# A streaming-encoder block: full-width moving parts beside retention, range sums on ScalarE, low weights three steps later

## The chip, the cores and the metric

The kernel runs on one core of a Trainium2 chip. The metric is the device time of one execution in microseconds (us). Three executions of the kernel before took 1543.58, 1543.76 and 1544.12 us; their median, 1543.76 us, is the time to compare with.

## What is computed

One layer over 512 tokens of width 2048: an RMS norm, one combined projection, a sparse attention mixer and a retention mixer, sigmoid gates, an output projection, a gated embedding and a last norm. What matters here is the middle of it:

```python
h = rmsnorm(x, norm_gain)
proj = h @ w_in
(aq, ak, av, az, iq, ik, iw, rq, rk, rv, rz, ga, gb) = jnp.split(proj, SPLIT_POINTS, axis=-1)
...
b_out = retention_mixer(rq, rk, rv, ret_gn_gain) * jax.nn.silu(rz)
merged = jax.nn.sigmoid(ga) * (a_out @ w_a_out) + jax.nn.sigmoid(gb) * (b_out @ w_b_out)
```

## The kernel before

Every large product is made in float16 from two-part numbers: a weight block `w` is split into a high part `wh` (ScalarE, line 257, with a scale) and a low part `wl` (VectorE, line 143: scaled `w` minus `wh`), and the input likewise into a high and a low half. The moving operand of a product is a tile of 512 columns, 256 of the high half beside 256 of the low half. `wh` multiplies all 512, `wl` the 256 high ones, and the two column halves of the result are added afterwards.

Two projections of 128 outputs each are computed together by `gemm_pair` with seven products in place of eight (a Strassen-like scheme: sums of weight blocks against sums of inputs). Four PSUM banks `v`, `p`, `q`, `r` collect the products. A pair has 14 runs of matmuls, 7 with `wh` and 7 with `wl`, each over 8 slices of the contraction. Runs with `wl` have 8 matmuls of 256 columns. Runs with `wh` have 8 matmuls of 512 columns, or, in a *compact* pair, 16 of 256: the high and the low half go one after the other into the same 256 columns of the bank.

What a pair leaves in PSUM is taken out in `copy` (ScalarE, line 372: a bank into SBUF) and `out` (VectorE). In a compact pair `out` is a single operation of 256 columns (line 1492 with its `done`), in any other it is one of 512 columns (line 378, tile `e_t`) and then one that adds the halves of `e_t` (line 1492):

```python
def out(f, x, y, i, c):
    if compact:
        return done(x[:, LO], y[:, LO], i, c, f)
    t = U("e_t")
    f(t, x, y)
    done(t[:, LO], t[:, HI], i, c)
```

The retention stage computes 8 heads. Each head has three pairs: the keys and queries of the head (called the first pair here), then two pairs of merge gates (the second and the third). `COMPACT = True, False, True` makes the first and the third compact. Beside them run the head's rotation (lines 1182 to 1189), its chunk states (line 1281) and its output norm, and rounds of the top-k search (lines 1082 and 1085) as background work. After the stage come sixteen pairs that are not compact.

The order of the work is written by hand: each engine runs its instructions in program order, and `step()`, called as the matmuls are issued, runs work that was put off with `later(n, f)`. `split_to` makes the next weight unit: it issues `wh` at once, and puts off `rest` (the low part, and a sum of weight blocks at line 268 or a DMA that adds one) by a lag of 1 step; there are three buffers each for `wh` and `wl`, and a unit is split shortly before it is used.

The low part of a weight also writes the sum of its row into a column of the tile `stats` (`accum_out`, in `low_part`). At the end `judge1` looks at the exponents of all columns, and a flag tells whether the values were in a range that the fast arithmetic can hold.

Of the kernel before, what the change touches and what calls it, by code (L numbers as in the profile page):

```python
# [59 lines left out]
    me = 2  # L60


STATS = 704
INDEX_Q = 2.0 ** -12
INDEX_K = 2.0 ** 6
LOGITS = 2.0 ** 10
SCALE_Q, SCALE_K, SCALE_V, SCALE_P = 128.0 ** -0.5 * 2.0 ** 7, 2.0 ** 3, 2.0 ** 3, 2.0 ** 14
EXP_LOW, EXP_HIGH = 124, 134
RET_QK, RET_V, RET_AT, RET_S = 2.0 ** 3, 2.0 ** 3, 2.0 ** -4, 2.0 ** -9
RET_Y = 2.0 ** 5  # L70

# [1 line left out]
def block_kernel(tc, flag, cfg, xT, pT, posb, posq, w_in, w_v, w_r0, w_r1, w_ik, w_a, w_b, w_o, w_ple, w_gate,  # L73
# [7 lines left out]
    with contextlib.ExitStack() as ctx:  # L81
# [41 lines left out]
        if fast:  # L123
            stats = cp.tile([128, STATS], F32, name="stats")
            pool.memset(stats, 1.0)
            one16 = cp.tile([128, 1], F16, name="one16")
            pool.memset(one16, 1.0)
        columns = [0]

        def column(n=1):  # L130
            c = slice(columns[0], columns[0] + n)
            columns[0] += n
            assert columns[0] <= STATS
            return stats[:, c]

        def low_part(l, src, h, gain=None, checked=False):
# [17 lines left out]
        loaded = {}  # L154
        raw_tiles = {}
        unfinished = {}
        state = {"raw": 0, "split": 0, "rate": BG_RATE, "hold": False, "owed": False, "banks": False, "turn": False, "lag": 1}
        in_raws, in_big, added, narrow_raws = set(), set(), set(), set()

        def raw(src, k0, nk, cols, plus=None):  # L160
            raws.append((src, k0, nk, cols, plus))
# [2 lines left out]
        def block(src, chunks, cols=128):  # L164
            ids, k0 = [], 0
            for nk in chunks:
                ids.append(len(units))
                units.append((raw(src, k0, nk, cols), None, nk, cols))
                k0 += nk
            return ids  # L170
# [44 lines left out]
        def view(t, nk, cols):  # L215
            return t.rearrange("p a c -> p (a c)")[:, 0:nk * cols].rearrange("p (a c) -> p a c", c=cols)
# [23 lines left out]
        def split_to(n, lag=None):  # L240
            lag = lag or state["lag"]
            while state["split"] < min(n, len(units)):
                i = state["split"]
                load_to(i + 1)
                r, plus, nk, cols = units[i]
                if r in unfinished:
                    unfinished[r]()
                raw = view(raw_tiles[r], nk, cols)
                if i in in_raws:
                    t = wp.tile([128, 2, 512], cfg.dt, name="whl", tag="wraw", bufs=cfg.raw_bufs)  # L250
                    h, l = t[:, 0:1], t[:, 1:2]
                elif nk * cols == L and i > u_ik[-1]:
                    h, l = (v.rearrange("p (a c) -> p a c", c=cols) for v in both("wh4", "wl4"))
                else:
                    h, l = (view(wp.tile([128, 8, 128], cfg.dt, name=n, tag=n), nk, cols) for n in ("wh", "wl"))
                if i > 0:
                    act.activation(h, raw, AF.Copy, scale=cfg.w)  # L257
                elif fast:
                    dve.tensor_scalar(h, raw, cfg.w, None, op0=OP.mult)
                else:  # L260
                    dve.tensor_copy(h, raw)

                def rest(r=r, plus=plus, l=l, raw=raw, h=h):
                    if unfinished.pop(r, None) is None:
                        return
                    low_part(l, raw, h, cfg.w if fast else None, True)
                    if isinstance(plus, int):
                        dve.tensor_add(raw, raw, view(raw_tiles[plus], nk, cols))  # L268
                    elif plus is not None:
                        later(ADD_LAG if r in in_big and r not in added else 0, lambda: add_block(r, plus))  # L270
                        added.add(r)

                unfinished[r] = rest
                later(lag, rest)
                loaded[i] = (h, l)
                state["split"] += 1
# [8 lines left out]
        def later(n, f):  # L285
            if n <= 0:
                return f()
            tick[1] += 1
            heapq.heappush(soon, (tick[0] + n, tick[1], f))
# [71 lines left out]
        def gemm_pair(ids, X, done, late=False, turned=False, nk=8, more=None, compact=False):  # L361
# [58 lines left out]
            for at, (n, part, ks) in enumerate(runs):  # L420
                at = max(at - early, 0) if late else at
                i, o = ids[n], banks[n]
                if more is not None:
                    more(at)
                elif at in SPLIT_AT and not (late and at == 2):
                    split_to(ids[0] + SPLIT_AT[at], (1 if state["turn"] else 5) if at == 2 else 1)
                if at in LOAD_AT and more is None:
                    load_to(ids[LOAD_AT.index(at)] + AHEAD + LOADS)
                if waiting and state["banks"] and 4 <= at <= 9:
                    bias_banks(waiting.popleft())  # L430
                w, c = loaded[i][part], (ALL, LO)[part]
                begin = ended[n] == 0
                for k in ks:
                    ended[n] += 1
                    x = X[PRODUCTS[n]][k]
                    if turned and isinstance(x, tuple):
                        moving = [(LO, v) for v in x[:2 - part]]
                    elif compact:
                        moving = [(LO, x[:, v]) for v in (LO, HI)[:2 - part]]
                    else:  # L440
                        moving = [(c, x[:, c])]
                    for j, (co, src) in enumerate(moving):
                        pe.matmul(o[:, co], w[:, k], src, start=(n < 4 and begin and k == 0 and j == 0),  # L443
                                  stop=(ended[n] == 2 * nk), skip_group_check=True)
                    count += 1
                    if count % (16 // nk) == 0:
                        step()
                if ended[n] == 2 * nk and n in after:
                    after[n]()
# [194 lines left out]
        PAIRED = [m + 8 * i for m in range(8) for i in range(2)]  # L644
        u_wa.update((m, block(w_a[m], (8,))) for m in PAIRED if m % 8 not in narrow and m not in u_wa)
        u_d = [block_pair(w_o[m], w_o[m + 8]) for m in range(8)]
        u_p = [block(w_ple[:, 8 * q:8 * q + 8], (8,)) for q in range(MF // 4)]
        u_e = [block(w_gate[m], K8) for m in range(cfg.me)]
        u_ep = [block_pair(w_gate[m], w_gate[m + 1]) for m in range(cfg.me, MF, 2)]
# [859 lines left out]
        for h in range(NH):  # L1509
            if fast and h == NH - 1:  # L1510
                state["rate"] = BG_RATES[3]
            if state["rate"] == BG_RATES[2]:
                later(38, lambda: hold(True))
                later(64, lambda: hold(False))
            if fast:
                for n in ROUNDS_IN_HEAD if h else ():
                    later(n, late_round)
            gate_pair(u_r[h], retention(h), COMPACT[0])
            for n in (2 * h, 2 * h + 1):
                d, m = ((sgb, 2 * n), (sga, 2 * n - 16))[n >= 8]  # L1520
                state["turn"] = fast and n == 2 * h
                gate_pair(u_g[n], to(d[m:m + 2], AF.Sigmoid), COMPACT[1 + n % 2])
        state["rate"] = BG_RATES[4]
        state["banks"] = True
        for n, u in enumerate(u_rz):
            y = B("y2")

            def b_out(i, o, y=y, n=n):
                act.activation(o, o, AF.Silu, scale=un_x)
                ov = o.rearrange("p (t i c) -> p t i c", t=4, i=4)  # L1530
                v = y[:, L * i:L * i + L].rearrange("p (i t c) -> p t i c", i=4, t=4)
                pool.tensor_mul(ov, ov, v)
                pool.dma_start(out=bd[2 * n + i], in_=o)

            def y_load(y=y, n=n):
                for i in range(2):
                    sp.dma_start(y[:, L * i:L * i + L], yd[2 * n + i])

            later(16 if n else 0, y_load)
            gate_pair(u, b_out)  # L1540
# [512 lines left out]
        def judge1():  # L2053
            e = cp.tile([128, STATS], I32, name="exps")
            dve.tensor_scalar(e, stats.bitcast(I32), 0x7F800000, 23, op0=OP.bitwise_and, op1=OP.logical_shift_right)
            n = F["n"] = [up.tile([128, 1024], F16, name=v, tag="u")[:, 0:STATS] for v in ("over", "good")]
            dve.tensor_scalar(n[0], e, float(EXP_HIGH), 1000.0, op0=OP.is_gt, op1=OP.mult)
            dve.scalar_tensor_tensor(n[1], e, float(EXP_LOW), n[0], op0=OP.is_ge, op1=OP.subtract)

        def judge2():  # L2060
            F["pe"] = [P("ps_e") for _ in range(2)]
# [151 lines left out]
RET_SPLITS = {("k", 0): 16, ("k", 1): 21, ("q", 0): 18, ("q", 1): 24, ("v", 0): 26, ("v", 1): 37,  # L2213
              ("vd", 0): 40, ("vd", 1): 45}
KEYS_AT = 30, 31
COMPACT = True, False, True
ROUNDS_AT = 19, 44
ROUNDS_IN_HEAD = 15, 44, 106, 106
QK_LOW = 5, 9
# [105 lines left out]
```

## Time and profile before

| what | value |
|---|---|
| median of three executions | 1543.76 us |
| the profiled execution, its own time | 1543.44 us |
| its span, from the first to the last instruction | 1541.6 us |
| TensorE matmul busy | 1529.4 us, 99% |
| VectorE busy | 1317.6 us, 85% |
| ScalarE busy | 970.0 us, 63% |
| GpSimd busy | 225.0 us, 15% |
| mean granted clock of TensorE | 0.998 |

The profile's page gives the busy time of each engine as a share of the span. A matmul's recorded duration is longer than the distance to the next one, because matmuls overlap; so distances between starts are read, not durations. The retention stage runs from about 248 to 706 us of the span.

### The profile page before, as it was taken

The numbers are of one execution on the slowest core, as the hardware profiler recorded it, in microseconds if no ns is written. First come the engines' busy times: TensorE is split into PE (matmuls) and PEld (weight loads), VectorE is DVE, ScalarE is ACT, GpSimd is POOL, SyncE is SP. The second block draws the span as 40 slices with busy tenths as digits, with TensorE's granted clock in tenths as the row PEclk, the third lists the DMA queues.
The fourth block names the chain that finished last, engine by engine and source line by source line (L and its number), as shares of the span: only waits on it lengthen the run. The fifth ranks groups of instructions, "written<-read, shape, count | busy, mean of one in ns | idle before, by whom it ended". The sixth has DMA issues, their size and how long they took to land.

```text
span 1541.6 us, 27918 instructions
## 1 busy us (share of the span) xinstructions
PE 1529.4 (99%) x10433; PEld 986.7 (64%) x10433; DVE 1317.6 (85%) x2712; ACT 970.0 (63%) x1491; POOL 225.0 (15%) x261
## 2 busy tenths in 40 slices
PE   9999999999999999999999999999999999999997
PEld 5654446778878878876555666655555566547765
DVE  8899889888888888987788888788889999998975
ACT  7565545665666665687877766667633555576654
POOL 3000111111111111113431121200000111101101
PEclk9999999999999999999999999999999999999999
DMA  8436989899899899899999898999556899878974
GB/s 325 134 117 196 263 213 253 227 228 236 219 227 237 216 228 235 217 228 268 272 248 243 229 249 239 276 352 343 198 198 191 209 232 241 221 232 238 259 213 147
DMA packets 136274, 358.26 MB, mean 232 GB/s; under 512 B 22208, under 2 KB 34752, under 8 KB 136128
## 3 DMA queue, kind: packets, MB, share of 16 engines
q1 hardware_dynamic: 94368, 230.08, 43.1%
q0 software_dynamic: 28656, 101.20, 35.4%
q10 hardware_dynamic: 13104, 25.09, 4.4%
q8 instruction: 83, 1.36, 0.3%
q14 instruction: 63, 0.52, 0.1%
HBM read 311.76 MB, written 42.99 MB: 230 GB/s over the span
## 4 chain that ended last, share of the span: by engine, by line
PE 88%; DVE 6%; ACT 2%; issue 1%; DMA 1%; SPq 0%; DVEq 0%; ACTq 0%
PE ps_p L443 27%; PE ps_v L443 18%; PE ps_q L443 9%; PE ps_r L443 9%; PE ps_vn L1151 2%; PE ps_vn L1150 2%; PE ps_vn L1152 2%; PE ps_iq L339 1%; PE ps_iq L337 1%; PE ps_iq L338 1%; DVE wl L143 1%; ACT bm L1610 1%; PE ps_pg L2018 1%; PE ps_pg L2019 1%; PE ps_pg L2020 1%
## 5 line engine op out<-in xcount | busy, mean ns | idle before, releaser
L143 DVE SCALAR_TENSOR_TENSOR wl<-wraw,wh 128x1024 f16<-128x1024 f32 (+3 forms) x461 | 559.1, 1221 | 124.4 <-ACT wh L257 113.5
L257 ACT ACTIVATE wh<-wraw 128x1024 f16<-128x1024 f32 (+3 forms) x484 | 490.1, 1024 | 136.1 <-DVE wraw L268 74.8
L443 PEld LDWEIGHTS <-wh 128*128 128x128 f16 x4120 | 402.2, 98 | 239.0 <-issue 1.5
L443 PEld LDWEIGHTS <-wl 128*128 128x128 f16 x2968 | 289.4, 98 | 55.0 <-issue 0.2
L221 POOL DMA_DIRECT2D wraw<-w_in x120 | 106.4, 969 | 562.3 <-DVE wl L143 479.8
L443 PE MATMUL ps_p<-hs,wh 128*128 128x256 f16 (+1 forms) x896 | 153.2, 318 | 0.0
L372 ACT ACTIVATE e<-ps_p 128x512 f32<-128x512 f32 (+1 forms) x158 | 83.3, 527 | 91.7 <-PE ps_p L443 85.1
L443 PE MATMUL ps_p<-hs,wl 128*128 128x256 f16 x640 | 84.2, 273 | 0.0
L443 PE MATMUL ps_q<-ha,wh 128*128 128x256 f16 (+1 forms) x448 | 76.0, 318 | 0.0
L443 PE MATMUL ps_r<-hs,wh 128*128 128x256 f16 (+1 forms) x448 | 75.9, 318 | 0.0
L443 PE MATMUL ps_v<-ha,wh 128*128 128x256 f16 (+1 forms) x448 | 75.9, 318 | 0.0
L443 PE MATMUL ps_p<-ha,wh 128*128 128x256 f16 (+1 forms) x448 | 75.9, 318 | 0.0
L443 PE MATMUL ps_v<-hs,wh 128*128 128x256 f16 (+1 forms) x448 | 75.9, 318 | 0.0
L1045 ACT ACTIVATE mk<-relf,thr 128x512 f16<-128x512 f32 (+3 forms) x128 | 67.5, 553 | 1.4 <-ACT go L1501 1.2
L268 DVE TENSOR_TENSOR wraw<-wraw 128x1024 f32<-128x1024 f32 x53 | 64.9, 1225 | 1.8
L339 PEld LDWEIGHTS <-wl 128*128 128x128 f16 x396 | 38.8, 98 | 40.8 <-DVE wl L143 0.9
L337 PEld LDWEIGHTS <-wh 128*128 128x128 f16 x396 | 38.9, 98 | 36.6
L338 PEld LDWEIGHTS <-wh 128*128 128x128 f16 x396 | 38.8, 98 | 36.6
L1501 ACT ACTIVATE go<-go 128x512 f32<-128x512 f32 x40 | 25.1, 629 | 51.3 <-DVE go L1492 51.3
L221 POOL DMA_DIRECT2D wraw<-w_o x24 | 21.0, 929 | 235.5 <-DVE wl L143 101.3
L338 PE MATMUL ps_w<-bh,wh 128*128 128x512 f16 x128 | 48.5, 379 | 0.0
L339 PE MATMUL ps_w<-bh,wl 128*128 128x512 f16 x128 | 48.5, 379 | 0.0
(471 smaller groups left out, 2858.0 us busy)
## 6 DMA issues: line engine op xcount, KB each, us to landing
wraw<-w_in SPq DMA_DIRECT2D x170, 512.0 KB, 5.5
wraw<-w_in POOLq DMA_DIRECT2D x120, 512.0 KB, 7.9
wraw<-w_o SPq DMA_DIRECT2D x32, 512.0 KB, 5.4
wraw<-w_o POOLq DMA_DIRECT2D x24, 512.0 KB, 7.6
wraw<-w_gate SPq DMA_DIRECT2D x24, 512.0 KB, 5.3
wraw<-w_v SPq DMA_DIRECT2D x16, 512.0 KB, 7.4
wraw<-w_b SPq DMA_DIRECT2D x16, 512.0 KB, 6.3
wraw<-w_gate POOLq DMA_DIRECT2D x15, 512.0 KB, 7.5
```

The lines of the kernel that those rows point to most:

```text
L143: dve.scalar_tensor_tensor(l, src, 1.0 if gain is None else gain, h, op0=OP.mult, op1=OP.subtract, **({"accum_out": column()} if checked a ...
L221: pool.dma_start(out=view(raw_tiles[r], nk, cols), in_=src[:, k0:k0 + nk, :], accum_op=OP.add)
L257: act.activation(h, raw, AF.Copy, scale=cfg.w)
L268: dve.tensor_add(raw, raw, view(raw_tiles[plus], nk, cols))
L337: pe.matmul(o, h[:, k, w], a, start=(s == order[0]), stop=False)
L338: pe.matmul(o, h[:, k, w], b, start=False, stop=False)
L339: pe.matmul(o, l[:, k, w], a, start=False, stop=(s == order[-1]))
L372: act.activation(E[n][:, cs], src[:, cs], AF.Copy)
L443: pe.matmul(o[:, co], w[:, k], src, start=(n < 4 and begin and k == 0 and j == 0), stop=(ended[n] == 2 * nk), skip_group_check=True)
L1045: act.activation(bias_e[b][i // per][:, ln * (i % per):ln * (i % per + 1)], relf[:, :ln], AF.Sign, bias=thr[:, q:q + 1])
L1150: pe.matmul(o, a[:, tok(t)], h[:, k], start=(s == 0), stop=False)
L1151: pe.matmul(o, a[:, tok(t)], l[:, k], start=False, stop=False)
```

## The change

In the retention stage no pair is compact any more: `COMPACT` becomes `False, False, False`. The row sums that watch the range of the stage's weights, 168 units from the first pair's first unit to the start of the next stage, are no longer taken with the low part on VectorE but with the high part on ScalarE (`accum_out` of the activation), into 168 columns at the end of `stats` of their own, which have other bounds in `judge1` and which a VectorE memset fills with 4096 at the start. In this stage the low part comes 3 steps behind the high one in place of 1, except at one place of each pair.

```diff
-STATS = 704
+STATS, HIGHS = 704, 168
...
-EXP_LOW, EXP_HIGH = 124, 134
+EXP_LOW, EXP_HIGH, EXP_UP = 124, 134, 11
...
             pool.memset(stats, 1.0)
+            dve.memset(stats[:, STATS - HIGHS:], 4096.0)
...
+                summed = fast and any(a <= i < b for a, b in summed_units)
                 if i > 0:
-                    act.activation(h, raw, AF.Copy, scale=cfg.w)
+                    act.activation(h, raw, AF.Copy, scale=cfg.w, **({"accum_out": column(1, 1)} if summed else {}))
...
-                    low_part(l, raw, h, cfg.w if fast else None, True)
+                    low_part(l, raw, h, cfg.w if fast else None, not summed)
...
-                    split_to(ids[0] + SPLIT_AT[at], (1 if state["turn"] else 5) if at == 2 else 1)
+                    split_to(ids[0] + SPLIT_AT[at], (1 if state["turn"] else 5) if at == 2 else state["low"])
...
+        summed_units += [(u_r[0][0], u_rz[0][0])]
...
+            state["low"] = LOW_LAG if fast else 1
             gate_pair(u_r[h], retention(h), COMPACT[0])
...
-            dve.tensor_scalar(n[0], e, float(EXP_HIGH), 1000.0, op0=OP.is_gt, op1=OP.mult)
-            dve.scalar_tensor_tensor(n[1], e, float(EXP_LOW), n[0], op0=OP.is_ge, op1=OP.subtract)
+            for c, by in ((slice(0, STATS - HIGHS), 0), (slice(STATS - HIGHS, STATS), EXP_UP)):
+                dve.tensor_scalar(n[0][:, c], e[:, c], float(EXP_HIGH + by), 1000.0, op0=OP.is_gt, op1=OP.mult)
+                dve.scalar_tensor_tensor(n[1][:, c], e[:, c], float(EXP_LOW + by), n[0][:, c], op0=OP.is_ge, op1=OP.subtract)
...
-COMPACT = True, False, True
+COMPACT = False, False, False
+LOW_LAG = 3
```

How the instructions stand on VectorE is shown at three places. Lines of the changed kernel are a few higher than those of the kernel before (381 for 378, 1496 for 1492, 144 for 143, 1191 for 1187, 663 for 659).

The first rows of VectorE's program, before and then with the change; `warm` is the operand of the matmuls that TensorE runs first:

```order
L2317 UNCONDITIONAL_BRANCH
L659 MEMSET warm 128x64
L661 MEMSET ones 128x128
L663 MEMSET mhalf 128x16
L665 MEMSET eps 128x1
```

```order
L2325 UNCONDITIONAL_BRANCH
L126 MEMSET stats 128x168
L663 MEMSET warm 128x64
L665 MEMSET ones 128x128
L667 MEMSET mhalf 128x16
L669 MEMSET eps 128x1
```

A memset of part of `stats` now stands ahead of that of `warm`; it writes over what GpSimd's memset of all of `stats` writes.

VectorE at the end of a first pair and the beginning of the second, in a head whose top-k round is 512 wide; `ct` and `rb` belong to the rotation, `wl` are low weights. Before, and with the change:

```order
L1085 MATCH_REPLACE isc<-m_4211,isc 128x512
L1492 TENSOR_TENSOR go<-ps_v,e_4311 128x256
L143 SCALAR_TENSOR_TENSOR wl,stats<-wraw,wh 128x1024
L1187 TENSOR_TENSOR go<-go,ct 128x512
L1188 TENSOR_TENSOR rb<-rb,st 128x512
L1189 TENSOR_TENSOR go<-go,rb 128x512
L1492 TENSOR_TENSOR go<-ps_p,pv 128x256
L1492 TENSOR_TENSOR go<-ps_r,e_4383 128x256
L143 SCALAR_TENSOR_TENSOR wl,stats<-wraw,wh 128x1024 x2
```

```order
L1089 MATCH_REPLACE isc<-m_4004,isc 128x512
L381 TENSOR_TENSOR e_t<-ps_v,e_4082 128x512
L1496 TENSOR_TENSOR go<-e_t 128x256
L144 SCALAR_TENSOR_TENSOR wl<-wraw,wh 128x1024
L1191 TENSOR_TENSOR go<-go,ct 128x512
L1192 TENSOR_TENSOR rb<-rb,st 128x512
L1193 TENSOR_TENSOR go<-go,rb 128x512
L381 TENSOR_TENSOR e_t<-ps_p,pv 128x512
L1496 TENSOR_TENSOR go<-e_t 128x256
L381 TENSOR_TENSOR e_t<-ps_r,e_4140 128x512
L1496 TENSOR_TENSOR go<-e_t 128x256
L144 SCALAR_TENSOR_TENSOR wl<-wraw,wh 128x1024 x2
```

Each of the three results now takes an operation of 512 columns ahead of the one of 256, and the low weights no longer write to `stats`; their place in the order is the same.

VectorE at the end of the second pair of that head, before and with the change:

```order
L1492 TENSOR_TENSOR go<-e_t 128x256
L143 SCALAR_TENSOR_TENSOR wl,stats<-wraw,wh 128x1024
L1082 MAX m_4579<-isc 128x8
L1085 MATCH_REPLACE isc<-m_4579,isc 128x256
L1259 TENSOR_TENSOR at<-ps_rs,dect 128x512
```

```order
L1496 TENSOR_TENSOR go<-e_t 128x256
L1086 MAX m_4338<-isc 128x8
L1089 MATCH_REPLACE isc<-m_4338,isc 128x256
L144 SCALAR_TENSOR_TENSOR wl<-wraw,wh 128x1024
L1263 TENSOR_TENSOR at<-ps_rs,dect 128x512
```

Here one low weight has moved behind a top-k round. In a steady head this is the one place where the lag of 3 steps changes VectorE's order.

## Rows read from the trace of the kernel before

**Rows 1.** What TensorE's matmuls waited for, whole span (us, times, longest).
```profile
PE ps_warm L703 <- DVE warm L659: 1.0, 1, 1.0
...
PE ps_p L443 <- ACT e L372: 0.4, 1, 0.4
```
**Rows 2.** Busy time by stretch: PE, PEld, DVE, ACT, POOL, PEclk, DMA share, GB/s.
```profile
363.03:381.37 18.34, 18.34 (x170) 16.44 (x168) 14.95 (x30) 10.55 (x15) 3.13 (x4) 1.00 0.98 256
381.37:400.24 18.87, 18.87 (x126) 11.63 (x124) 17.83 (x34) 13.08 (x18) 2.65 (x3) 1.00 0.84 206
400.24:420.26 20.02, 20.02 (x200) 18.12 (x199) 16.70 (x42) 11.09 (x17) 3.26 (x4) 1.00 0.85 219
...
858.91:877.11 18.20, 18.20 (x113) 10.95 (x112) 15.74 (x31) 13.62 (x24) 2.65 (x3) 1.00 0.90 228
```
**Rows 3.** Timeline of the first 6 us: start, duration, engine, instruction.
```profile
0.73 0.69 POOL L125 MEMSET stats<- 128x704 f32 x1 [0.29 <-POOLq L2312]
...
0.82 0.11 DVE L659 MEMSET warm<- 128x64 uint32 x1 [0.82 <-PEq L2312]
0.91 0.17 DVE L661 MEMSET ones<- 128x128 f32 x1
...
0.99 4.66 PE L703 MATMUL ps_warm<-warm 128*128 128x512 bf16 x11 [0.99 <-DVE warm L659]
...
5.49 0.38 PE L324 MATMUL ps_ikw<-hh,wh 128*128 128x512 f16 x1
```
**Rows 4.** What weight loads waited for, 0 to 250 us (us, times, longest).
```profile
PEld L339 <- DVE wl L143: 0.9, 2, 0.5
```
**Rows 5.** VectorE's timeline in one head's first two pairs, and near the end.
```profile
377.69 1.23 DVE L143 SCALAR_TENSOR_TENSOR wl<-wraw,wh 128x1024 f16<-128x1024 f32 x1 [1.80 <-ACT wh L257]
...
379.51 0.42 DVE L1492 TENSOR_TENSOR go<-ps_v,e 128x256 f32<-128x256 f32 x1
...
383.20 0.42 DVE L1492 TENSOR_TENSOR go<-ps_p,pv 128x256 f32<-128x256 f32 x1
...
383.86 1.22 DVE L143 SCALAR_TENSOR_TENSOR wl<-wraw,wh 128x1024 f16<-128x1024 f32 x1
...
385.95 1.23 DVE L143 SCALAR_TENSOR_TENSOR wl<-wraw,wh 128x1024 f16<-128x1024 f32 x1 [0.87 <-ACT rb L1183]
...
393.73 1.22 DVE L143 SCALAR_TENSOR_TENSOR wl<-wraw,wh 128x1024 f16<-128x1024 f32 x1
394.87 0.08 DVE L143 DVE_READ_ACCUMULATOR wl<-wraw,wh 128x1 f32 x1
394.87 1.22 DVE L143 SCALAR_TENSOR_TENSOR wl<-wraw,wh 128x1024 f16<-128x1024 f32 x1
...
401.98 0.68 DVE L378 TENSOR_TENSOR e_t<-ps_p,pv 128x512 f32<-128x512 f32 x1
402.70 0.42 DVE L1492 TENSOR_TENSOR go<-e_t 128x256 f32<-128x256 f32 x1
...
1506.21 0.89 DVE L2058 SCALAR_TENSOR_TENSOR good<-exps,over 128x704 f16<-128x704 int32 x1
```
**Rows 6.** ScalarE's groups by form, whole span: busy us, mean ns of one.
```profile
L372 ACT ACTIVATE e<-ps_p 128x512 f32<-128x512 f32 x110 | 64.9, 590 | 57.8 <-PE ps_p L443 54.4 <-ACT pw L1909 1.6 <-ACT go L1501 0.8
...
L372 ACT ACTIVATE e<-ps_p 128x256 f32<-128x256 f32 x48 | 18.4, 384 | 33.9 <-PE ps_p L443 30.7 <-ACT go L1501 3.2
...
L1610 ACT ACTIVATION_READ_ACCUMULATOR bm<-bm,nm 128x1 f32 x32 | 6.0, 187 | 0.0
```
**Rows 7.** TensorE's timeline: four runs that need what VectorE or ScalarE makes.
```profile
384.82 1.04 PE L443 MATMUL ps_v<-hs,wl 128*128 128x256 f16 x8
...
396.10 0.38 PE L443 MATMUL ps_v<-ha,wl 128*128 128x256 f16 x2
...
464.95 1.26 PE L443 MATMUL ps_r<-hs,wh 128*128 128x256 f16 x10
...
1508.66 0.46 PE L2063 MATMUL ps_e<-good,one 128*1 128x512 f16 x2
```
**Rows 8.** ScalarE's timeline in another head's third pair.
```profile
463.07 1.06 ACT L257 ACTIVATE wh<-wraw 128x1024 f16<-128x1024 f32 x1 [0.46 <-PE ps_kv L1207]
```

More of the change, by code (lines that the diff above doesn't have):

```diff
@@ L125, in block_kernel, with column @@
             pool.memset(stats, 1.0)
+            dve.memset(stats[:, STATS - HIGHS:], 4096.0)
             one16 = cp.tile([128, 1], F16, name="one16")
             pool.memset(one16, 1.0)
[L128 to L133, printed above, removed]
+        columns = [0, STATS - HIGHS]
+        def column(n=1, of=0):
+            c = slice(columns[of], columns[of] + n)
+            columns[of] += n
+            assert columns[of] <= (STATS - HIGHS, STATS)[of]
             return stats[:, c]
@@ L156, in block_kernel @@
         unfinished = {}
-        state = {"raw": 0, "split": 0, "rate": BG_RATE, "hold": False, "owed": False, "banks": False, "turn": False, "lag": 1}
+        state = {"raw": 0, "split": 0, "rate": BG_RATE, "hold": False, "owed": False, "banks": False, "turn": False, "lag": 1, "low": 1}
         in_raws, in_big, added, narrow_raws = set(), set(), set(), set()
+        summed_units = []
         def raw(src, k0, nk, cols, plus=None):
@@ L261, in split_to, with rest @@
                     dve.tensor_copy(h, raw)
-                def rest(r=r, plus=plus, l=l, raw=raw, h=h):
+                def rest(r=r, plus=plus, l=l, raw=raw, h=h, summed=summed):
                     if unfinished.pop(r, None) is None:
                         return
-                    low_part(l, raw, h, cfg.w if fast else None, True)
+                    low_part(l, raw, h, cfg.w if fast else None, not summed)
                     if isinstance(plus, int):
@@ L1524, in block_kernel @@
         state["banks"] = True
+        state["low"] = 1
         for n, u in enumerate(u_rz):
```

## Prediction

> **What bounds the kernel now.** I read the waits of TensorE first. Over the whole span its matmuls waited in four places, and the only wait in the retention stage that the view names is 0.4 us long; the longest, 1.0 us, is the start [rows 1]. So TensorE is issued without a gap, and the time is the number and the spacing of its matmuls. The stretches say the same: in each pair PE is busy for all of it [rows 2]. They also show what is nearest to becoming a limit. In one head the three pairs last 18.34, 18.87 and 20.02 us, and VectorE works 14.95, 17.83 and 16.70 of them. That leaves it 3.4, 1.0 and 3.3 us. ScalarE has 7.8, 5.8 and 8.9 us left.
>
> **What the change gives.** The first pair of a head holds nothing but its 14 runs and is compact: 18.34 us. A pair that was never compact, with the same products, takes 18.20 [rows 2]. The columns are the same; the compact pair has 56 matmuls more. So a compact pair costs 0.14 us more, and 16 of them (two in each of 8 heads) give back **2.3 us** (16 x 0.146 with one more digit, 2.6 ns for each of 896 matmuls). This is sure as long as nothing makes TensorE wait.
>
> **The start.** The new memset stands first on VectorE and must wait until GpSimd has filled `stats`, at 0.73 + 0.69 = 1.42 us; behind it waits the memset of `warm`, at 0.82 before, and behind that TensorE's first matmul, at 0.99 [rows 3]. A memset of 128 columns takes 0.17 at most, so 168 take some 0.2. `warm` is written near 1.6, and TensorE begins 0.8 us late. Its eleven first matmuls then run as before up to the first of the real work (5.49 before), so all of it is 0.8 late. Some is won back: two weight loads waited for low weights later, 0.9 us in all [rows 4], and those waits shrink when TensorE comes later. The matmuls lose less than the loads, so I take 0.2 of it, between 0 and 0.8. **+0.6 us**, between 0 and 0.8.
>
> **VectorE's added work.** Each of four results of a formerly compact pair gets an operation of 512 columns ahead of that of 256. From the start of one to the dependent one behind it is 0.72 us (401.98 to 402.70 [rows 5]), so 2.9 us for a pair that had 3.4 or 3.3 idle. That fits on the average but leaves nothing, so I follow the queue through the head of [rows 5].
>
> A first pair comes to rest at 377.69, where a low weight waits for ScalarE. Behind it three results are taken out, at 379.51, at 383.20 and just after: 3 x 0.72 = 2.16 us more. At 385.95 a low weight had waited 0.87 us. The view names `rb`, but the run of low-weight matmuls that frees its buffer begins at 384.82 and ends at 385.86 [rows 7], just ahead; so I take it that TensorE ended the wait, and that it swallows 0.87. 1.29 us remain, and from there VectorE has 1.0 us idle in the whole second pair.
>
> Two smaller shifts stand against each other. ScalarE's copy ahead of 377.69 becomes 0.21 longer (590 against 384 ns [rows 6]), its accumulator read adds up to 0.19, and TensorE releases it 0.10 earlier (five of the pair's seven high runs are done): +0.1 to +0.3. The accumulator reads that leave VectorE are recorded with 0.08 each, but the next low weight starts where the read does (394.87 [rows 5]), so five of them on this path give 0 to 0.4. I set both to 0.2. **The queue is 1.3 us late**, between 1.0 and 1.6.
>
> The low weight at 393.73 is ready at 394.95, and its run starts at 396.10 [rows 7], 0.14 earlier after the gain above: 1.0 us to spare. TensorE waits 0.3 us in each head, 2.4 with this rounding, 2.2 without it: **+2.2 us**, between 0 and 4.6.
>
> The second place is the third pair's fourth unit. ScalarE makes its high weight behind the activation of the second pair's last result, which the same queue delays. In the tightest head it is ready at 463.07 + 1.06 = 464.13 [rows 8] for a run at 464.95 [rows 7]: 0.8 to spare, 0.2 less for TensorE's gain, 0.3 more for the stall just counted. Late by 1.3, it costs 0.4 us. The three widths of the top-k round take turns, so I count it for two heads of eight: **+0.8 us**, between 0 and 3.2.
>
> **Edits at nothing.** On ScalarE 21 high weights a head get a read of at most 0.19 and eight copies become 0.21 longer: 5.7 us against 22.5 idle. If that cover failed, the high weights would come late as in the second place. The lag of 3 steps puts one low weight a head behind a top-k round; that weight is for the next pair's low runs, two full runs of high ones away. It moves no DMA on GpSimd's or SyncE's queue past another; the adding DMAs behind a low weight start as late as that weight. The two operations added to the judgement lie ahead of 1508.66, where TensorE needs `good`, ready at 1507.10 [rows 5, 7]; even at 0.89 us for both they fit into the 1.56 between.
>
> **Sum.** -2.3 + 0.6 + 2.2 + 0.8 = +1.3 us: a span of 1542.9, 1544.7 for the profiled execution (1543.44, which stands 0.3 below the median) and **1545.1 us** against the median of 1543.76. A change of 0.2%, 3.1 us, is about what a measurement of this kernel can tell from none.
>
> **Rivals.**
> *No stall.* The shifts on VectorE's queue fall out low, 1.0 late or less, and only the start is lost: -2.3 + 0.6 = -1.7, 1542.1 us. For it: VectorE's total still fits, and pairs of the next stage, with VectorE busy for 15.74 of 18.20 us [rows 2], ran with no wait. Against it: the second pair has no reserve.
>
> *The gap travels (slower).* The wait before 385.95 was for `rb`, as the view names it. `rb` waits for the last result, moves with it, and swallows nothing. Then the queue is 2.16 late; TensorE waits 2.16 - 1.01 = 1.15 us in each head, 9.2 in all, and the second place keeps its 0.8: -2.3 + 0.6 + 9.2 + 0.8 = +8.3, 1552.1 us. It decides from the point where less than 0.87 is swallowed. For it: the named releaser. Against it: the 0.09 us between the run's end and the start.
>
> *The start is free.* The memset waits for nothing on the path, or its delay vanishes in the two waits: 0.6 less, 1544.5 us.
>
> *The clock rises elsewhere.* The eleven first matmuls took (5.49 - 0.99) / 11 = 0.41 us each [rows 3], against 18.20 / 84 = 0.22 for 512 columns later [rows 2]: the lower of TensorE's two levels, 1.2 GHz, then 2.4. If the rise keeps its moment although the work begins 0.8 later, 0.8 us of half-rate work is saved and the start costs 0.4 less: 1544.7 us. If it comes a whole such stretch later, 4.5 us of work run at half rate and 2.2 are lost: 1547.3 us. The Trainium skill's page "TensorE: Matmul & The Clock Gate", section "What's actually happening", says that the monitor runs freely and does not begin anew with a kernel, so that the moment depends on where the first matmul lands. By that rule the rise need not move with the start; this trace has one start and shows neither.
>
> **How the numbers follow.** The forecast has 0.45, no stall 0.28, the travelling gap 0.15, the clock 0.07, a free start 0.05. Within the forecast's case the bounds of the two stalls reach from -1.7 to +6.1; above +3.1 I put 0.10 of its 0.45. Slower by over 0.2%: 0.10 + 0.15 + 0.02 of the clock's case = 0.27. No case gives more than 2.3 us, so faster by over 0.2% gets 0.03 for what I have not seen, and the same 0.70. The range takes in no stall below and most of the forecast's upper bound, 1541.5 to 1549.0; the travelling gap lies outside.
>
> **What would show it.** Right: TensorE's first matmul near 1.8 us with VectorE's memset of `stats` ahead of `warm`; first pairs of 18.20 us; a wait of some 0.3 us in the second pair of each head, by a load of `wl` for line 143; VectorE idle by some 2 us a head. The no-stall case shows no such wait. The travelling gap shows over 1 us a head, and VectorE still idle ahead of the low weight behind the rotation. Wrong altogether: a first pair that keeps 18.34, or waits for something other than VectorE and ScalarE.

## The result

The changed kernel takes **1554.18 us** (median of six executions, 1553.77 to 1555.88) against 1544.03 us for the kernel before on the same chip (six executions, 1543.58 to 1544.95). The ratio is 1.007, 95% interval 1.0059 to 1.0081: slower by 10 us. The prediction said 1545.1 us, within 1541.5 to 1549.0, so the sign of its sum was right, and the sum was 9 us too small.

### The profile page after: what moved, and what is told of

Its sections match the earlier page's. It is cut to its first block, busy times and chain, and to the rows that moved or that the text cites. A ratio compares the mean times of both kernels' runs of the same rounds, so it can differ in the third digit from the quotient of the medians.

```text
span 1552.0 us, 26190 instructions
## 1 busy us (share of the span) xinstructions
PE 1531.8 (99%) x9537; PEld 896.3 (58%) x9537; DVE 1356.5 (87%) x2611; ACT 993.3 (64%) x1659; POOL 223.9 (14%) x261
## 4 chain that ended last, share of the span: by engine, by line
PE 65%; DVE 22%; ACT 8%; issue 4%; DMA 1%; ACTq 1%; SPq 0%; DVEq 0%; POOL 0%; POOLq 0%
PE ps_p L446 18%; PE ps_v L446 12%; DVE wl L144 6%; PE ps_r L446 6%; PE ps_q L446 5%; DVE e_t L381 3%; ACT wh L260 3%; PE ps_vn L1155 2%; PE ps_vn L1154 2%; PE ps_vn L1156 2%; DVE go L1496 2%; PE ps_iq L340 1%; PE ps_iq L341 1%; PE ps_iq L342 1%; DVE wraw L271 1%
## 5 line engine op out<-in xcount | busy, mean ns | idle before, releaser
L446 PEld LDWEIGHTS <-wh 128*128 128x128 f16 x3224 | 313.4, 98 | 319.7 <-ACT wh L260 14.0
L446 PEld LDWEIGHTS <-wl 128*128 128x128 f16 x2968 | 287.6, 98 | 73.6 <-DVE wl L144 10.1
L446 PE MATMUL ps_p<-hs,wh 128*128 128x512 f16 x640 | 152.5, 379 | 0.0
L375 ACT ACTIVATE e<-ps_p 128x512 f32<-128x512 f32 x158 | 92.9, 588 | 52.8 <-PE ps_p L446 43.6
L446 PE MATMUL ps_r<-hs,wh 128*128 128x512 f16 x320 | 75.7, 379 | 3.7 <-ACT wh L260 3.6
L446 PE MATMUL ps_v<-ha,wh 128*128 128x512 f16 x320 | 75.6, 379 | 0.1
L446 PE MATMUL ps_q<-ha,wh 128*128 128x512 f16 x320 | 75.7, 379 | 0.0
L446 PE MATMUL ps_v<-hs,wh 128*128 128x512 f16 x320 | 75.6, 379 | 0.0
L446 PE MATMUL ps_p<-ha,wh 128*128 128x512 f16 x320 | 75.6, 379 | 0.0
L1496 DVE TENSOR_TENSOR go<-e_t 128x256 f32<-128x256 f32 x160 | 68.0, 425 | 5.8
L340 PEld LDWEIGHTS <-wh 128*128 128x128 f16 x396 | 38.8, 98 | 36.8
L341 PEld LDWEIGHTS <-wh 128*128 128x128 f16 x396 | 38.7, 98 | 36.6
```

The source lines that it names most:

```text
L340: pe.matmul(o, h[:, k, w], a, start=(s == order[0]), stop=False)
L341: pe.matmul(o, h[:, k, w], b, start=False, stop=False)
L375: act.activation(E[n][:, cs], src[:, cs], AF.Copy)
L1496: f(o[:, q], c0, c1)
```

## The profile after

The busy times and the shares of the chain that ended last, from the page of the changed kernel (span 1552.0 us):

```profile
PE 1531.8 (99%) x9537; PEld 896.3 (58%) x9537; DVE 1356.5 (87%) x2611; ACT 993.3 (64%) x1659; POOL 223.9 (14%) x261
...
PE 65%; DVE 22%; ACT 8%; issue 4%; DMA 1%; ACTq 1%; SPq 0%; DVEq 0%; POOL 0%; POOLq 0%
```

PE is still "99% busy". The shares of busy time hardly tell the two kernels apart. The chain does. Before, TensorE carried 88% of it and VectorE 6%; now VectorE carries 22% and ScalarE 8%. The line of the page before:

```profile
PE 88%; DVE 6%; ACT 2%; issue 1%; DMA 1%; SPq 0%; DVEq 0%; ACTq 0%
```

The waits say the same. Here is what TensorE's matmuls and then its weight loads waited for in the retention stage (248 to 717 us; us in total, times, longest), where the matmuls of the kernel before waited for nothing that the view names (the 0.4 us of [rows 1] lies at 1164.28 us, behind the stage):

```profile
PE ps_r L446 <- ACT wh L260: 3.6, 9, 1.0
PE ps_p L446 <- ACT rq L1202: 1.7, 3, 0.8
PE ps_v L446 <- DVE wl L144: 1.3, 7, 0.2
PE ps_p L446 <- DVE wl L144: 0.2, 1, 0.2
...
PEld L446 <- ACT wh L260: 12.7, 24, 1.5
PEld L446 <- DVE wl L144: 9.5, 16, 1.1
```

A load's wait is longer than that of its matmuls: at 371.33 the load waited 0.90 us and the matmul 0.41. The matmul's wait of 1.7 us "for rq" is one for a low weight: at the same places the load's row names `wl` (393.45, below). What TensorE really loses I take from the distances between matmul starts, beyond 0.216 us for 512 columns and 0.109 for 256. In the stage that is 11.9 us in five places, beside single gaps of 0.05 us. "Run 5" counts the 14 runs of a pair from 0.

| place | needs | lost, all heads | forecast |
|---|---|---|---|
| first pair, run 5 | fourth high weight | 4.1 us | nothing |
| first pair, run 8 (last head) | fifth low weight | 0.4 us | nothing |
| second pair, run 8 | fifth low weight | 3.1 us | nothing |
| second pair, run 11 (in the last head also run 10) | sixth low weight (run 10: sixth high weight) | 2.7 us | 2.2 us |
| third pair, run 5 | fourth high weight | 1.6 us | 0.8 us |

The stretches that answer to [rows 2], in the same head (columns as there):

```profile
363.84:382.62 18.78, 18.37 (x114) 10.86 (x113) 17.62 (x28) 10.80 (x20) 3.75 (x4) 1.00 0.95 238
382.62:402.30 19.68, 19.22 (x126) 11.48 (x125) 19.24 (x30) 14.23 (x26) 2.65 (x3) 1.00 0.84 218
402.30:422.18 19.88, 19.88 (x144) 12.65 (x143) 17.48 (x36) 12.40 (x24) 2.64 (x3) 1.00 0.87 220
```

The third pair fell from 20.02 to 19.88 us: the gain as forecast. The first pair should have fallen to 18.20 and took 18.78, the second 19.68 in place of 18.87. VectorE is busy for 19.24 us of the second.

**The wait that was not foreseen.** ScalarE at the beginning of that first pair, before:

```profile
362.68 0.63 ACT L1501 ACTIVATE go<-go 128x512 f32<-128x512 f32 x1 [1.89 <-DVE go L1492]
...
363.72 0.38 ACT L372 ACTIVATE e<-ps_p 128x256 f32<-128x256 f32 x1 [0.40 <-ACT go L1501]
364.00 1.05 ACT L257 ACTIVATE wh<-wraw 128x1024 f16<-128x1024 f32 x1
364.94 0.62 ACT L1501 ACTIVATE go<-go 128x512 f32<-128x512 f32 x1
...
366.02 1.06 ACT L257 ACTIVATE wh<-wraw 128x1024 f16<-128x1024 f32 x1 [0.46 <-ACT go L1501]
...
376.61 1.05 ACT L257 ACTIVATE wh<-wraw 128x1024 f16<-128x1024 f32 x1
```

The same instructions after the change (the pair begins at 363.84 in place of 363.03):

```profile
365.00 0.63 ACT L1505 ACTIVATE go<-go 128x512 f32<-128x512 f32 x1 [2.79 <-DVE go L1496]
...
366.16 0.60 ACT L375 ACTIVATE e<-ps_p 128x512 f32<-128x512 f32 x1 [0.54 <-PE ps_v L446]
366.66 1.05 ACT L260 ACTIVATE wh<-wraw 128x1024 f16<-128x1024 f32 x1
...
369.04 0.63 ACT L1505 ACTIVATE go<-go 128x512 f32<-128x512 f32 x1 [1.24 <-DVE go L1496]
...
370.13 1.06 ACT L260 ACTIVATE wh<-wraw 128x1024 f16<-128x1024 f32 x1 [0.46 <-ACT go L1505]
371.09 0.19 ACT L260 ACTIVATION_READ_ACCUMULATOR wh<-wraw 128x1 f32 x1
...
378.47 1.04 ACT L260 ACTIVATE wh<-wraw 128x1024 f16<-128x1024 f32 x1
```

And VectorE in the changed kernel, which those rows wait for (its last row, like the last rows of the two fences above, is read further down):

```profile
363.82 0.68 DVE L381 TENSOR_TENSOR e_t<-ps_v,e 128x512 f32<-128x512 f32 x1
364.54 0.43 DVE L1496 TENSOR_TENSOR go<-e_t 128x256 f32<-128x256 f32 x1
...
366.79 0.69 DVE L381 TENSOR_TENSOR e_t<-ps_p,pv 128x512 f32<-128x512 f32 x1 [0.69 <-ACT e L375]
367.52 0.42 DVE L1496 TENSOR_TENSOR go<-e_t 128x256 f32<-128x256 f32 x1
367.86 0.69 DVE L381 TENSOR_TENSOR e_t<-ps_r,e 128x512 f32<-128x512 f32 x1
368.58 0.43 DVE L1496 TENSOR_TENSOR go<-e_t 128x256 f32<-128x256 f32 x1
...
377.38 3.49 DVE L144 SCALAR_TENSOR_TENSOR wl<-wraw,wh 128x1024 f16<-128x1024 f32 x3
```

The results taken out there are the third pair's last ones. The work goes from VectorE (first result) to ScalarE (its sigmoid, then the copy `e` behind it) back to VectorE (two results) and again to ScalarE (the second sigmoid), and only behind that does ScalarE's program have the fourth high weight. So all three operations of 512 columns lie in one chain, 3 x 0.72 = 2.16 us, with 0.21 for the longer copy. Counted from the start of the pair, the first result comes 0.78 us later than before and the high weight is ready at 7.35 in place of 4.05 us, while TensorE wants it at 6.9. Its accumulator read ends at 371.28, 7.44 us after the pair's start, and the run starts just behind that, with 0.57 us lost:

```profile
371.33 1.47 PE L446 MATMUL ps_r<-hs,wh 128*128 128x512 f16 x6 [0.41 <-ACT wh L260]
```

**The second pair.** What the forecast took from [rows 5] looks like this now. First VectorE:

```profile
387.98 2.35 DVE L144 SCALAR_TENSOR_TENSOR wl<-wraw,wh 128x1024 f16<-128x1024 f32 x2
...
392.18 1.22 DVE L144 SCALAR_TENSOR_TENSOR wl<-wraw,wh 128x1024 f16<-128x1024 f32 x1
```

Then the loads of low weights:

```profile
393.45 0.77 PEld L446 LDWEIGHTS <-wl 128*128 128x128 f16 x8 [0.56 <-DVE wl L144]
...
398.14 0.11 PEld L446 LDWEIGHTS <-wl 128*128 128x128 f16 x2 [0.67 <-DVE wl L144]
```

Two low weights stand back to back at 387.98: the wait of 0.87 us between them is gone, swallowed as forecast. But the low weight behind the rotation (389.04 before, 392.18 now) comes 9.56 us after the pair's start in place of 7.67, 1.9 later, and its run had 1.5 us to spare. The run at 398.14 is the one that was forecast. It loses 0.34 us in each of seven heads. That the loss is the same in each has a reason that the forecast did not have. From the fifth low weight to the sixth VectorE takes 4.68 us (392.18 to 396.86; 4.69 before, 389.04 to 393.73). TensorE needs 4.33 us from run 8 to run 11 (8 x 0.109 and 16 x 0.216). So once run 8 waits, run 11 loses the difference, however late the queue is.

## The experiments

Theory A: the added operation of 512 columns for each result makes VectorE late, and through ScalarE's order the high weights too. Theory B: the range sums on ScalarE make the high weights late. Theory C: the lag of 3 makes the low weights late. Twelve kernels ran; times are medians, "stage" is the profiled time from the first matmul of the first head to the first one of the next stage (before 457.80 us, changed 467.99 us). "Lost" is counted from the distances, as above.

### One part at a time

Full-width parts alone, in the kernel before:

```diff
-COMPACT = True, False, True
+COMPACT = False, False, False
```

> The kernel before with full-width moving parts in all pairs of the retention stage and nothing else changed (range sums stay on VectorE, lag 1, no memset). Theory A (the extra operation of 512 columns for each result makes VectorE late, and through ScalarE's waits for VectorE the high weights too): most of the loss is here, 1550 to 1554 us, TensorE waits in the first pair's run 5 and in the second pair's runs 8 and 11. Theory B (ScalarE's range sums make the high weights late) and theory C (the lag of 3 makes the low weights late): only the gain of 2.3 us is left, about 1541.7 us.

Lag 1 in the changed kernel:

```diff
-LOW_LAG = 3
+LOW_LAG = 1
```

> The changed kernel with a lag of 1 step in place of 3. Theory A: within 1.5 us of the changed kernel, 1552.7 to 1555.7 us. Theory B: the same. Theory C: the ten microseconds go, 1542 to 1544 us.

Compact pairs in the changed kernel:

```diff
-COMPACT = False, False, False
+COMPACT = True, False, True
```

> The changed kernel with compact first and third pairs again (range sums on ScalarE, lag 3 and the early memset stay). Theory A: the waits go and the gain with them, 1543 to 1546 us. Theories B and C: the waits stay and the gain of 2.3 us goes, 1555 to 1557 us.

Full-width parts with a lag of 3, in the kernel before:

```diff
...
-                    split_to(ids[0] + SPLIT_AT[at], (1 if state["turn"] else 5) if at == 2 else 1)
+                    split_to(ids[0] + SPLIT_AT[at], (1 if state["turn"] else 5) if at == 2 else state["low"])
...
+            state["low"] = 3 if fast else 1
...
-COMPACT = True, False, True
+COMPACT = False, False, False
```

> The kernel before with full-width moving parts and a lag of 3 in the retention stage; range sums stay on VectorE, no memset. Theory A: as with the full-width parts alone, within 1.5 us of that run, 1550 to 1554 us. Theory B: 1541.7 us. Theory C: 1553 to 1555 us while the run with lag 1 has 1541.7 us.

| kernel | us | ratio to before (95%) | stage | lost in the stage |
|---|---|---|---|---|
| full width alone | 1551.88 | 1.0054 (1.0040 to 1.0068) | 465.52 | 9.6 |
| changed, lag 1 | 1555.09 | 1.0076 (1.0062 to 1.0090) | 468.09 | 12.0 |
| changed, compact pairs | 1544.34 | 1.0003 (0.9994 to 1.0012) | 457.80 | 0.0 |
| full width, lag 3 | 1551.57 | 1.0052 (1.0038 to 1.0066) | 466.00 | 10.1 |

Theory A holds. Full width alone costs 7.7 us of the stage's 10.2; with compact pairs, range sums and lag cost the stage nothing. The lag gives nothing (stage 468.09 with 1, 467.99 with 3; with the sums on VectorE 465.52 and 466.00, 0.5 us more). Theory B has a part that only shows with full width: the sums on ScalarE add 2.0 us at a lag of 3 (467.99 less 466.00) and 2.6 at a lag of 1 (468.09 less 465.52), most of it in the two runs that need high weights (first pair 3.1 to 4.1, third 1.0 to 1.6). The group of these reads in the changed kernel:

```profile
L260 ACT ACTIVATION_READ_ACCUMULATOR wh<-wraw 128x1 f32 x168 | 32.0, 191 | 0.0
```

### The added operation itself, and whose results

The changed kernel with one operation for each result of the first and the third pairs, as in a compact pair, so that the columns of the low half are left out of these results (`one` is set for these pairs; the lines that hand it on are not shown):

```diff
-                if compact:
+                if compact or one:
                     return done(x[:, LO], y[:, LO], i, c, f)
```

> The changed kernel without the extra operation: in the formerly compact pairs VectorE takes out only the columns of the high half, so the other half of these sums is left out of the output. Matmuls, ScalarE's copies of 512 columns, range sums, lag and memset stay as changed. Theory A: all waits go and the gain of 2.3 us is there: 1541.3 to 1543 us. Rival (the longer copies and the reads on ScalarE make the weights late): 1546 us or more.

It took 1541.62 us (0.9988, 0.9979 to 0.9997), and its stage 455.56 us, 2.24 less than before. The stretches of the head (the windows have the lengths of its pairs and stand 0.43 us behind their first matmuls, 362.59, 380.79 and 399.66):

```profile
363.02:381.22 18.20, 18.20 (x113) 10.97 (x112) 14.76 (x22) 12.05 (x23) 3.04 (x5) 1.00 0.98 250
381.22:400.09 18.87, 18.87 (x125) 11.63 (x124) 18.11 (x31) 13.91 (x26) 2.64 (x3) 1.00 0.87 222
400.09:419.97 19.88, 19.88 (x144) 12.60 (x142) 16.28 (x32) 12.13 (x24) 3.36 (x4) 1.00 0.85 216
```

Nothing waits, with 512-column matmuls, longer copies, sums, lag and memset all in place. So the term of the gain, 2.3 us, is whole, and no wait comes without the added operation of VectorE: putting it in costs 467.99 - 455.56 = 12.4 us. (The five places hold 11.9 of it; the rest are gaps of 0.05 us and less.) The share of the sums on ScalarE, 2.0 to 2.6 us, lies within these 12.4: it comes only where the operation has made the weights late. This kernel computes less and is no candidate.

The third pair full alone, and the first pair full alone, in the kernel before:

```diff
-COMPACT = True, False, True
+COMPACT = True, False, False
```

> The kernel before with full-width moving parts in the third pair of each head only. Its gain is half, 1.2 us (8 pairs of 0.146). Theory A1 (the third pair's results, taken out at the start of the next head's first pair, pass twice from VectorE to ScalarE ahead of that pair's fourth high weight): TensorE waits in the first pair's run 5, 2 to 3.5 us in all, and nowhere in the second pair, since the first pair's results are short: 1544.4 to 1546.0 us. Rival (only the first pair's results matter, because VectorE comes to rest behind the third pair's): no wait, 1542.4 us.

```diff
-COMPACT = True, False, True
+COMPACT = False, False, True
```

> The kernel before with full-width moving parts in the first pair of each head only; gain 1.2 us. Theory A1: no wait in the first pair; the queue of the second pair is then late by its own three results alone, 2.16 us less the wait of 0.87, so run 11 loses 0.3 us in each head, 2.4 us, and run 8 little: 1544.4 to 1545.4 us. Rival (the second pair's waits do not need the third pair's results): runs 8 and 11 lose 5 us as with all pairs full, 1547 to 1548 us.

The third alone took 1543.52 us (0.9998, 0.9989 to 1.0007), its stage 457.03 us, and I had expected it slower. One run in the whole stage lost 0.3 us. ScalarE there, in a pair that begins at 363.44:

```profile
365.10 0.60 ACT L372 ACTIVATE e<-ps_p 128x512 f32<-128x512 f32 x1 [0.40 <-ACT go L1501]
...
369.06 1.06 ACT L257 ACTIVATE wh<-wraw 128x1024 f16<-128x1024 f32 x1 [0.46 <-PE ps_p L443]
```

The high weight is ready 6.68 us after the pair's start, 2.63 later than before; TensorE needs it at 6.98. Of these 2.63 us the chain is 2.37 (2.16 and 0.21), and the first result comes 0.25 later than before. That eats 2.6 of the 2.9 us that were to spare and stops just short.

The first alone took 1545.24 us (1.0011, 1.0002 to 1.0020), stage 459.44. It lost 1.9 us in the second pair's run 11, 0.12 to 0.35 in a head, and 0.6 in the third pair's run 5, and nothing in run 8. What the weight loads waited for there:

```profile
PEld L443 <- DVE wl L143: 4.5, 8, 0.7
PEld L443 <- ACT wh L257: 1.5, 4, 0.4
```

These are the two places and nearly the sizes that the forecast gave for the whole change. So the two pairs' losses do not add: 0.3 and 2.5 us apart, 9.6 together with nothing else changed. In this head the third pair's first result is taken out at -0.02 us from the first pair's start with all pairs full, at -0.55 with the third alone, and at -0.80 both before and with the first alone. So the first pair's results alone leave nothing behind at the head's end; only with the third pair's results do they hand on 0.5 us more, and that is more than the 0.3 us that the chain had left. At which place of the head the two join was not tried apart.

### Taking the waits away

ScalarE's sigmoid of the merge gates 12 steps behind its result in place of 1, in the changed kernel, so that each sigmoid stands behind the high weight that it stood ahead of:

```diff
-                    later(1, lambda: finish(i, o))
+                    later(lag, lambda: finish(i, o))
...
-                gate_pair(u_g[n], to(d[m:m + 2], AF.Sigmoid), COMPACT[1 + n % 2])
+                gate_pair(u_g[n], to(d[m:m + 2], AF.Sigmoid), COMPACT[1 + n % 2], 12)
```

> The changed kernel with ScalarE's sigmoid of the merge gates 12 steps later, behind the high weight that it now stands ahead of. Theory A (ScalarE's order makes it wait for VectorE's late result): the 4.1 us in the first pair's run 5 and most of the 1.6 us in the third pair's go, the waits in the second pair (5.7 us) shrink by 0 to 2: 1546.5 to 1549 us. Rival (VectorE itself is full, whatever ScalarE's order is): the waits move to low weights, 1552 us or more.

It took 1546.21 us (1.0015, 1.0006 to 1.0024), 0.3 below what was expected; its stage is 461.18. No run 5 waits any more, in the first or the third pair; the second pair still loses 2.9 us in run 8 and 2.4 in runs 10 and 11. So some 6.8 of the 10.2 us were ScalarE's place in the order, with VectorE's work unchanged. ScalarE in that kernel, in a pair that begins at 364.65:

```profile
364.85 0.60 ACT L375 ACTIVATE e<-ps_p 128x512 f32<-128x512 f32 x1 [2.06 <-PE ps_p L446]
365.35 1.05 ACT L260 ACTIVATE wh<-wraw 128x1024 f16<-128x1024 f32 x1
...
366.39 0.62 ACT L1505 ACTIVATE go<-go 128x512 f32<-128x512 f32 x1
...
367.46 1.06 ACT L260 ACTIVATE wh<-wraw 128x1024 f16<-128x1024 f32 x1 [0.46 <-ACT go L1505]
```

The copy waits for TensorE alone, and the high weight is ready 3.9 us after the pair's start in place of 7.35.

Three versions on the kernel before (sums on VectorE, lag 1), each with this later sigmoid: the third pair full; the first pair full, with the second operation of the second pair's results on GpSimd; and all pairs full, with the second operation of the second and third pair's results on GpSimd. The last one's edit beside the later sigmoid, where `add` comes from `gate_pair`:

```diff
-            def done(c0, c1, i, q, f=dve.tensor_add):
+            def done(c0, c1, i, q, f=add or dve.tensor_add):
...
-                gate_pair(u_g[n], to(d[m:m + 2], AF.Sigmoid), COMPACT[1 + n % 2])
+                gate_pair(u_g[n], to(d[m:m + 2], AF.Sigmoid), COMPACT[1 + n % 2], 12, pool.tensor_add)
...
-COMPACT = True, False, True
+COMPACT = False, False, False
```

> The kernel before with full-width moving parts in the third pair only and the sigmoid of the merge gates 12 steps later. Theory A: the 0.3 us that TensorE still waited with the third pair full goes, the gain of 1.2 us stays whole: 1542.4 us, and a retention stage of 456.6 us. Rival (the later sigmoid makes something else late): 1543 us or more, with a wait that names ScalarE.

> The kernel before with the first pair full, the sigmoid 12 steps later, and the add of halves of the second pair's results on GpSimd. With the first pair full alone TensorE waited 1.9 us in run 11 of the second pair and 0.6 in run 5 of the third. Theory A: the add that stood ahead of run 11's low weight is gone from VectorE, some 0.4 us against waits of 0.12 to 0.35, and the third pair's high weight no longer stands behind the sigmoid; no wait is left: 1542.4 us, stage 456.6 us. Rival (VectorE loses as much elsewhere): 1544 us or more.

> The kernel before with all pairs full, the sigmoid 12 steps later, and the second operation (the add of the two halves) of the second and third pair's results on GpSimd. VectorE gets 2.3 us less in a head's second and third pair results each. Theory A: hardly any wait is left, at most 0.3 us in the second pair's run 11: 1541.5 to 1543.5 us. Rival (GpSimd's order: its adds stand ahead of the scale of the output norm, for which VectorE waits in the first pair): waits in the first or second pair, 1544 us or more.

| kernel | us | ratio to before (95%) | stage |
|---|---|---|---|
| third full, later sigmoid | 1542.97 | 0.9995 (0.9986 to 1.0004) | 456.78 |
| first full, later sigmoid, adds on GpSimd | 1543.06 | 0.9996 (0.9987 to 1.0005) | 456.82 |
| all full, later sigmoid, adds on GpSimd | 1541.57 | 0.9987 (0.9978 to 0.9996) | 456.00 |

The stages of the first two come 0.2 us from what was expected, though their medians stand 0.6 and 0.7 us above it and can't be told from no change. The third is faster than both kernels, by 2.0 us against the kernel before and, by the two ratios, by some 13 us against the changed one. Its matmuls wait for nothing in the stage that the view names (by the distances 0.3 us are lost in the second pair's run 8), and the loads for little:

```profile
PEld L443 <- DVE wl L143: 1.2, 5, 0.4
PEld L443 <- ACT wh L257: 0.6, 2, 0.4
```

### The start

The changed kernel with VectorE's memset of `stats` behind the other four:

```diff
-            dve.memset(stats[:, STATS - HIGHS:], 4096.0)
...
         dve.memset(eps, EPS)
+        if fast:
+            dve.memset(stats[:, STATS - HIGHS:], 4096.0)
```

> The changed kernel with VectorE's memset of the columns of stats behind the four other memsets at the start, so that TensorE begins near 1.0 us as before. The forecast's start term: 0.6 us less than the changed kernel (0 to 0.8), 1553.4 to 1554.2 us. Rival (the clock's rise sets when the first real matmul comes, so that the late begin costs nothing in the mean): no less than the changed kernel, 1554.2 us or more.

It took 1553.87 us (1.0065, 1.0051 to 1.0079), stage 467.97. That is 0.3 us less than the changed kernel's median of another series, too little to decide between 0 and 0.6.

## Why the prediction was wrong

**The gain, -2.3 us: right.** 2.24 where nothing waits, and full pairs of 18.20 and 19.88 us.

**The start, +0.6 us: right in its rows; its size is perhaps half of that, and not well known.** The memset stands where it was said, and the work begins 0.86 us later:

```profile
0.73 0.68 POOL L125 MEMSET stats<- 128x704 f32 x1 [0.29 <-POOLq L2320]
...
1.52 0.20 DVE L126 MEMSET stats<- 128x168 f32 x1 [1.52 <-POOL one L128]
1.68 0.11 DVE L663 MEMSET warm<- 128x64 uint32 x1
...
1.85 4.16 PE L707 MATMUL ps_warm<-warm 128*128 128x512 bf16 x11 [1.85 <-DVE warm L663]
...
5.85 0.38 PE L327 MATMUL ps_ikw<-hh,wh 128*128 128x512 f16 x1
```

Of the 0.86 us, 0.36 arrive at the first real matmul ([rows 3] has it at 5.49), and none at the stage, which begins at 248.56 (248.58 before). Over the profiles of all kernels the stage began at 248.39 to 249.27 where TensorE started at 0.99 (nine profiles, median 248.55), and at 248.56 to 249.74 where it started at 1.85 (five, median 248.86): some 0.3 us by the medians, with ranges that overlap.

**VectorE's queue in the second pair, +2.2, and the fourth unit of the third pair, +0.8: right for another kernel.** They measure 2.7 and 1.6 in the changed kernel, and 1.9 and 0.6 in the one with only the first pair full, which is what was worked out. That 2.7 lies near 2.2 is in part luck: in the changed kernel the size comes from VectorE's 4.68 us against TensorE's 4.33, and not from a queue that is 1.3 us late.

**The step that failed** is the sentence "A first pair comes to rest at 377.69, where a low weight waits for ScalarE", from which the queue was followed as if nothing had happened before it. The third pair's three results got no price at all, as if the 1.80 us of rest ahead of 377.69 swallowed them; that the first pair's fourth high weight stands behind them on ScalarE was not looked at, though the same place of the third pair was. Two things follow from that. First, they pass twice between VectorE and ScalarE ahead of a high weight with 2.9 us to spare and take 2.4 of it; with the lateness of the first result and the reads on ScalarE, that is 4.1 us in run 5. Secondly, the rest is gone: three low weights run back to back there (377.38 to 380.87). The first of them starts 13.5 us after the pair's start in place of 10.5 (373.51 before), so VectorE arrives 3.1 us late at a rest of 1.80. The end of the rest has moved as well: the high weight that it waited for, at 376.61, now starts at 378.47, 14.6 us after the pair's start in place of 13.6, behind two others that wait for VectorE's sum of blocks (line 268, now 271) and start at 12.1 in place of 9.4. The first pair's first result is taken out 0.68 us later against the pair's end than before, so the second pair's low weights are 1.9 us late in place of 1.3, and run 8, with 1.5 us to spare, loses 3.1 us in the eight heads.

The three places that the forecast had at nothing lose 7.6 us, of the 8.8 by which its +1.3 fell short of the measured 10.1. With the terms as measured the sum is -2.3 + 0.3 + 11.9 = 9.9 us.

**"On ScalarE 21 high weights a head get a read ... 5.7 us against 22.5 idle" at nothing: wrong in this kernel, right in the other.** With compact pairs the sums cost the stage 0.0; where the high weights are already late, the reads count, 2.0 to 2.6 us in all. An average idle share did not cover it. The lag at nothing was right for the changed kernel (0.1 us less than with a lag of 1).

**The rivals.** The travelling gap gave 1552.1 us, near the result, but it fell: its 0.87 us was swallowed, as 387.98 shows. The right number would have been for the wrong reason. No stall fell too. "The clock rises elsewhere" holds in that the rise does not follow the start (below); with the same start the stage began at 248.56 in one profile and at 249.74 in another, so that neither of its two prices is the one to take.

**A reading that was wrong without harm.** The prediction puts the wait of 0.4 us in [rows 1] into the retention stage. The row lies at 1164.28 us; in the stage the matmuls waited for nothing that the view names, which only strengthens what it was read for.

## What to carry to other kernels

Follow a queue around a whole period of the loop, not from the point where it last idled: a rest in the trace of before ends when another engine's work is ready, and both of its ends can move. Where two engines hand results to each other in program order, count how many times a chain crosses before it reaches what the bound engine needs; here two crossings put three added operations into one chain, while the busy shares (87% and 64%) showed nothing. And when the work fits but comes late, first move what stands ahead of the late instruction without need: here the later sigmoid gave back two thirds of the stage's 10.2 us, without any work taken away.

## What the runs showed of the hardware

**The clock's rise is not tied to the start.** The eleven first matmuls took from 3.68 to 4.67 us in five kernels with the same start at 1.85 us. At the 0.42 us each of the lower level (1.2 GHz) and 0.22 of the upper one (2.4 GHz), the shortest puts the rise near 4.5 us (an estimate: 6.3 matmuls of 0.42). In two other kernels with that start the first real matmul still ran for 0.63 us at 6.5, so the rise came later. That scatter of over 2 us is wider than the 0.86 by which the work moved. The Trainium skill, page "TensorE: Matmul & The Clock Gate", section "What's actually happening", says that the monitor runs freely and isn't reset by a kernel's start; these traces agree.

**A GpSimd add slows VectorE.** GpSimd takes 1.30 us on average for an add of 256 columns (0.72 to 1.70) where VectorE takes 0.43, and it is not free beside VectorE. The kernel with the adds on GpSimd, by group (us busy, mean ns):

```profile
L143 DVE SCALAR_TENSOR_TENSOR wl<-wraw,wh 128x1024 f16<-128x1024 f32 x441 | 558.0, 1276 | 84.7 <-ACT wh L257 84.1
...
L1492 POOL TENSOR_TENSOR go<-e_t 128x256 f32<-128x256 f32 x64 | 80.2, 1300 | 150.0 <-DVE e_t L378 101.3
```

With full width alone the same 441 low weights took 535.7 us, 1227 ns each. So 64 adds of 0.43 us, 27 us, left VectorE (1.7 us for each pair, not the 2.3 of the expectation), and 22 us came back in longer low weights. (Low weights that overlap no such add took 1.22 us in that kernel too.) One such pair of rows:

```profile
394.57 1.64 POOL L1492 TENSOR_TENSOR go<-e_t 128x256 f32<-128x256 f32 x1 [10.69 <-DVE e_t L378]
...
395.55 1.75 DVE L143 SCALAR_TENSOR_TENSOR wl<-wraw,wh 128x1024 f16<-128x1024 f32 x1
```

The low weight took 0.53 us more than its usual 1.22, beside an add that was still running. The Trainium skill, page "SBUF — State Buffer", section "SBUF: two separate sides", says that a VectorE operation with two inputs in SBUF and a GpSimd operation that reads SBUF lock each other out of a shared port for a whole instruction; the row agrees that they hinder each other, though it does not show a lock for the add's full length. The waits went all the same. Which part of that came from the adds' place in the queue and which from the sums being back on VectorE was not tried apart.
